# An encoder trunk on one core: the feed-forward activation transposed by Vector in one instruction per block, with SBUF-to-SBUF transfers to the quadrants

## The chip, the cores and the metric

The kernel runs on one core of a Trainium2 chip. The metric is the device time of one execution in microseconds (us), as the median over runs; a span is the time that the hardware profiler shows between the first and the last instruction of one profiled execution.

## The reference

Two layers over 256 tokens of width 2048, all in float32. Each layer is a token mixer with four kinds of heads (differential attention, convolution, grouped-query attention, neighbourhood attention) followed by a dense SwiGLU channel mixer. The change touches the channel mixer alone:

```
for l in range(DEPTH):                      # DEPTH = 2
    ...                                     # token mixer, x = x + rmsnorm(mixed)
    h = rmsnorm(x, norm_ffn_pre[l])         # x is 256 x 2048
    f = (silu(h @ ffn_gate[l]) * (h @ ffn_up[l])) @ ffn_down[l]   # hidden width 5632
    x = x + rmsnorm(f, norm_ffn_post[l])
```

The product with `ffn_down` contracts over the hidden width, so the activation `silu(gate) * up`, which comes out with tokens on the partitions, has to stand with hidden channels on the partitions before it can be a stationary operand of TensorE.

## The kernel before, in words

**Precision.** Every float32 product is made of three single-pass products: an operand is split into a high part (rounded) and a low part (the rest). ScalarE writes the high part (`whi`, `xT`, `hT`) and VectorE the low part by a subtraction (`wlo` and the second half of `xT`, `hT`). So one step, a `Step` of `products`, is six matmuls of 128 x 512 columns on two PSUM banks, and each weight tile passes through ScalarE and VectorE once.

**Units and groups.** `plan` cuts each big product into units of 128 rows by 1024 columns of weights. Two units come by one load of 1 MB into one of `NRAW` = 3 raw buffers; in the phase "gu" (gate and up) a load is two transfers of 512 KB, one from `ffn_gate` and one from `ffn_up`. Split units live in `NSPLIT` = 7 buffers `hi` and 7 buffers `lo`. Units are used in groups, four at a time as a rule: four steps for the first 128 tokens (tok 0), then the same four units for the other 128 (tok 1). A split buffer comes free with a tok-1 step. A column block of 512 hidden channels, j, is 16 units, that is 32 steps. There are 11 blocks per layer.

**Order.** Nothing reorders the program: each engine runs its instructions as the Python code emits them. `run` emits step by step: first `tick`, which advances every open generator whose planned time has come by one `yield`, then `splits_to`, which emits the splits up to 7 units beyond the units that are used up, and after every second low part the load that goes into the raw buffer which that low part was the last to read. Loads go out on SP's queue.

**Around the change.** When the last step of block j for one tok is emitted, `ffn_half` is spawned. ScalarE applies SiLU to the gate's bank (`h`), VectorE multiplies by the up bank (`h`), then `quadrants` is called four times with a `yield` after each: four VectorE transposes of 32 partitions by 128 columns a time, each of which swaps 32 x 32 blocks and writes them to another quadrant of partitions, into `ht`. After the fourth, `split_hi_lo` writes `hT[j]`: the high part by ScalarE, the low part by VectorE. `hT[j]` is read in the phase "down", which goes through the units in the order of j. The tiles `h` and `ht` come from a pool with 4 buffers.

**Transfers in the program.** The transfer of `gains` (`constants`, on ScalarE's queue) is the first of the program; on SP follow `x`, a weight load, `x`, two weight loads, two of `x`, and then the weight load that is the ninth. `load_bias` issues 16 transfers of 64 KB in a row on SP, once per layer; its destinations are separate parts of one tile.

Of the kernel before, what the change touches and what calls it, by code (L numbers as in the profile page):

```python
# [19 lines left out]
P = 128  # L20
# [30 lines left out]
class Unit:  # L51


    def __init__(self, phase, pair, k, raw, half):
        self.phase, self.pair, self.k, self.raw, self.half = phase, pair, k, raw, half
        self.hi = self.lo = None
# [46 lines left out]
class Trunk:  # L103
    def __init__(self, ctx, tc, a):
        self.tc, self.a = tc, a
        self.nc = Engines(self, tc.nc)
        self.at = {"PE": 0.0, "ACT": 0.0, "DVE": 0.0, "Pool": 0.0}
        self.chain = 0.0
        self.table = None
        self.made = {}  # L110
        pool = lambda name, bufs, **kw: ctx.enter_context(tc.tile_pool(name=name, bufs=bufs, **kw))
        self.cp = pool("consts", 1)
        self.wp = pool("weights", NSPLIT)
        self.sp = pool("slots", SLOTS)
        self.tp = pool("temps", 4)
        self.pacc = pool("acc", 4, space=PSUM)
        self.psc = pool("scores", 2, space=PSUM)
        self.ptp = pool("transposes", 2, space=PSUM)
        self.pd = pool("spill", 1, space=DRAM)
        self.open = {"sc": 0, "tp": 0}  # L120
        self.gens = []
        self.units, self.raws, self.steps = [], [], []
        self.next_raw = self.next_split = self.next_lo = 0
        self.conv_work = None
        self.xT = [None] * 4
        self.x = [None] * T
        self.acc = {}
        self.uid = 0
# [286 lines left out]


    def square_sum(self, src, out, n=(512,), bias=0.0):
        junk = self.tp.tile([P] + list(n), mybir.dt.bfloat16, tag="junk", bufs=2, name=self.name("junk"))
        self.nc.scalar.activation(junk, src, AF.Square, bias=bias, accum_out=out)

    def transpose_x(self, phase, tok, c):
# [109 lines left out]
    def ffn_half(self, phase, j, tok):  # L531
        nc = self.nc
        gate, up = (self.acc[phase, j, tok, b] for b in range(2))
        h = self.tmp([512], "h")
        r = self.rstd[:, tok:tok + 1]
        nc.scalar.activation(h, gate, AF.Silu, scale=r)
        nc.vector.scalar_tensor_tensor(h, up, r, h, op0=ALU.mult, op1=ALU.mult)
        yield
        if tok == 0:
            self.hT[j] = self.slot([2, 4, S], F32R, "hT")  # L540
        t = self.tmp([4, P], "ht")
        for q in range(4):
            self.quadrants(t, h.rearrange("p (k n) -> p k n", k=4), q)
            yield
        self.split_hi_lo([self.hT[j][:, i, :, tok * P:(tok + 1) * P] for i in range(2)], t)
        self.mark("h", phase[1], j, tok)

    def quadrants(self, dst, src, q):

        qs = slice(32 * q, 32 * q + 32)  # L550
        for r in range(4):
            rs = slice(32 * r, 32 * r + 32)
            self.nc.vector.transpose(dst[qs, :, rs], src[rs, :, qs])


    def layer_consts(self, l):
# [600 lines left out]
```

## Time and profile before

| what | value |
|---|---|
| median of 3 runs | 2179.1 us (2178.68 to 2179.65) |
| the profiled execution, its own time | 2179.21 us |
| its span | 2177.4 us |
| granted TensorE clock, mean | 0.999 of full speed |
| PE busy | 2156.2 us, 99% |
| DVE busy | 1459.9 us, 67% |
| ACT busy | 1083.2 us, 50% |
| bytes moved | 424.46 MB, 195 GB/s |

How to read it: PE is TensorE's matmuls, PEld its weight loads, DVE is VectorE, ACT ScalarE, POOL GpSimd, SP SyncE, and SPq SP's queue of transfers. A line "a<-b" gives the tile written and the tiles read. What stands in brackets behind a row of a timeline is how long the engine had been idle before it and for whom it waited. All lines of the helper that wraps the engines appear as L89.

### The profile page before, as it was taken

The numbers are of one execution on the slowest core, as the hardware profiler recorded it, in microseconds if no ns is written. First come the engines' busy times: TensorE is split into PE (matmuls) and PEld (weight loads), VectorE is DVE, ScalarE is ACT, GpSimd is POOL, SyncE is SP. The second block draws the span as 40 slices with busy tenths as digits, with TensorE's granted clock in tenths as the row PEclk, the third lists the DMA queues.
The fourth block names the chain that finished last, engine by engine and source line by source line (L and its number), as shares of the span: only waits on it lengthen the run. The fifth ranks groups of instructions, "written<-read, shape, count | busy, mean of one in ns | idle before, by whom it ended". The sixth has DMA issues, their size and how long they took to land.

```text
span 2177.4 us, 25660 instructions
## 1 busy us (share of the span) xinstructions
PE 2156.2 (99%) x9720; PEld 1780.7 (82%) x9720; DVE 1459.9 (67%) x2202; ACT 1083.2 (50%) x1420; POOL 28.7 (1%) x38
## 2 busy tenths in 40 slices
PE   8999999999999999999999999999999999999998
PEld 6888887888888888888878888878888888888886
DVE  5898555777777777444468975556677777764444
ACT  5556754544444444343465576554444444443432
POOL 0000000000000000000000000000000000000000
PEclk9999999999999999999999999999999999999999
DMA  7556446655555555555575553556555655555553
GB/s 281 197 173 181 171 148 222 210 196 193 193 194 194 193 194 194 213 193 194 211 238 186 188 186 135 208 189 222 193 191 180 209 193 193 179 208 213 193 216 132
DMA packets 170013, 424.46 MB, mean 195 GB/s; under 512 B 18593, under 2 KB 19105, under 8 KB 167585
## 3 DMA queue, kind: packets, MB, share of 16 engines
q1 hardware_dynamic: 169744, 422.79, 56.5%
q8 instruction: 76, 1.25, 0.2%
q14 instruction: 49, 0.39, 0.1%
q10 hardware_dynamic: 144, 0.03, 0.0%
HBM read 414.40 MB, written 8.39 MB: 194 GB/s over the span
## 4 chain that ended last, share of the span: by engine, by line
PE 96%; ACT 2%; DVE 1%; DMA 1%; issue 1%; SPq 0%; DVEq 0%; POOLq 0%; ACTq 0%
PE acc L89 92%; PE tp L89 3%; PE sc L89 1%; DMA raw<-in_w_in_dram 1%; ACT whi L89 1%; ACT workA L89 0%; ACT L89 0%; DVE xT L89 0%; DVE mx L89 0%; DVE wlo L89 0%; DVE x L89 0%; ACT xT L89 0%; ACT conv L89 0%; ACT qkD L89 0%; ACT junk L89 0%
## 5 line engine op out<-in xcount | busy, mean ns | idle before, releaser
L89 PE MATMUL acc<-whi,xT 128*128 128x512 f32 x4096 | 1292.9, 393 | 7.4 <-DVE xT L89 2.9
L89 PEld LDWEIGHTS acc<-whi,xT 128*128 128x128 f32 x4096 | 769.3, 188 | 172.3 <-DVE xT L89 5.5
L89 PE MATMUL acc<-wlo,xT 128*128 128x512 f32 x2048 | 798.7, 390 | 0.5 <-DVE wlo L89 0.5
L89 DVE SCALAR_TENSOR_TENSOR wlo<-raw,gains,whi 128x1024 fp32r<-128x1024 f32 x512 | 641.4, 1280 | 146.9 <-ACT whi L89 141.2
L89 ACT ACTIVATE whi<-raw,gains 128x1024 fp32r<-128x1024 f32 x512 | 574.7, 1147 | 269.6 <-PE acc L89 243.1
L89 DVE TENSOR_TENSOR wlo<-raw,whi 128x1024 fp32r<-128x1024 f32 x240 | 293.3, 1224 | 256.9 <-ACT whi L89 240.1
L89 PEld LDWEIGHTS acc<-wlo,xT 128*128 128x128 f32 x2048 | 385.1, 188 | 78.4 <-DVE wlo L89 1.0
L89 PE MATMUL acc<-whi,hT 128*128 128x512 f32 x1408 | 434.1, 389 | 0.0
L89 ACT ACTIVATE whi<-raw 128x1024 fp32r<-128x1024 f32 x240 | 253.6, 1060 | 296.1 <-PE acc L89 295.2
L89 PEld LDWEIGHTS acc<-whi,hT 128*128 128x128 f32 x1408 | 264.3, 188 | 54.9
L89 PE MATMUL acc<-wlo,hT 128*128 128x512 f32 x704 | 273.9, 389 | 0.0
L89 DVE STREAM_TRANSPOSE ht<-h 32x128 f32<-32x128 f32 x704 | 213.1, 303 | 10.9
L89 PEld LDWEIGHTS acc<-wlo,hT 128*128 128x128 f32 x704 | 132.1, 188 | 27.3
L89 ACT ACTIVATE hT<-ht 128x512 fp32r<-128x512 f32 x44 | 27.8, 632 | 244.3 <-DVE ht L89 244.3
L89 DVE SCALAR_TENSOR_TENSOR h<-acc,rstd,h 128x512 f32<-128x512 f32 x44 | 32.9, 747 | 110.8 <-ACT h L89 110.7
L89 DVE SCALAR_TENSOR_TENSOR conv<-uT,lc,conv 128x256 f32<-128x256 f32 x240 | 99.2, 477 | 0.0
L89 ACT ACTIVATE h<-acc,rstd 128x512 f32<-128x512 f32 x44 | 30.3, 688 | 81.6 <-PE acc L89 81.3
L89 DVE TENSOR_TENSOR hT<-ht,hT 128x512 fp32r<-128x512 f32 x44 | 30.4, 692 | 26.6 <-ACT hT L89 26.5
L89 ACT ACTIVATE junk<-acc 128x512 bf16<-128x512 f32 x32 | 19.1, 596 | 55.4 <-PE acc L89 53.3
L89 DVE TENSOR_TENSOR mg<-acc,gpost 128x512 f32<-128x512 f32 x32 | 21.4, 686 | 36.0 <-PE acc L89 19.3
L89 PE MATMUL acc<-whi,mixC 128*128 128x512 f32 x128 | 44.7, 402 | 0.0
L89 DVE TENSOR_TENSOR xT<-tp,xT 128x512 fp32r<-128x512 f32 x32 | 22.0, 687 | 30.2 <-ACT xT L89 30.2
(136 smaller groups left out, 992.0 us busy)
## 6 DMA issues: line engine op xcount, KB each, us to landing
raw<-in_ffn_gate_dram SPq DMA_DIRECT2D x176, 512.0 KB, 3.9
raw<-in_ffn_up_dram SPq DMA_DIRECT2D x176, 512.0 KB, 4.8
raw<-in_ffn_down_dram SPq DMA_DIRECT2D x88, 1024.0 KB, 4.9
raw<-in_w_in_dram SPq DMA_DIRECT2D x63, 1024.0 KB, 5.1
raw<-in_w_out_dram SPq DMA_DIRECT2D x32, 1024.0 KB, 5.0
raw<-in_w_in_dram SPq DMA_DIRECT2D x34, 512.0 KB, 4.8
x_spill<-x SPq DMA_DIRECT2D x6, 1024.0 KB, 7.7
x<-x_spill SPq DMA_DIRECT2D x6, 1024.0 KB, 8.4
```

The source lines that it names most:

```text
L89: return f(*args, **kw)
```

## The change

The 16 transposes per block and tok become one. It transposes each 32 x 32 block where it stands, on all 128 partitions, into a new tile `blocks` laid out by destination quadrant. Then SP issues 16 transfers, each of 32 partitions by 512 bytes (16 KB), from quadrant t of `blocks` to quadrant q of `ht`. Eight further ticks pass before the split. `ht` now has the layout (t, k, n) and the split reads it through a rearranged view. The pool `temps` gets 5 buffers in place of 4, and the scratch tile `junk` of the sums of squares 1 in place of 2.

```
-        self.tp = pool("temps", 4)
+        self.tp = pool("temps", 5)
...
-        junk = self.tp.tile([P] + list(n), mybir.dt.bfloat16, tag="junk", bufs=2, name=self.name("junk"))
+        junk = self.tp.tile([P] + list(n), mybir.dt.bfloat16, tag="junk", bufs=1, name=self.name("junk"))
...
         t = self.tmp([4, P], "ht")
-        for q in range(4):
-            self.quadrants(t, h.rearrange("p (k n) -> p k n", k=4), q)
-            yield
-        self.split_hi_lo([self.hT[j][:, i, :, tok * P:(tok + 1) * P] for i in range(2)], t)
+        yield from self.turned(t, h)
+        t = t.rearrange("p t (k n) -> p k t n", k=4)
+        dst = [self.hT[j][:, i, :, tok * P:(tok + 1) * P].rearrange("p k (t n) -> p k t n", t=4) for i in range(2)]
+        self.split_hi_lo(dst, t)
         self.mark("h", phase[1], j, tok)
 
-    def quadrants(self, dst, src, q):
-
-        qs = slice(32 * q, 32 * q + 32)
-        for r in range(4):
-            rs = slice(32 * r, 32 * r + 32)
-            self.nc.vector.transpose(dst[qs, :, rs], src[rs, :, qs])
+    def turned(self, dst, src):
+
+        nc = self.nc
+        b = self.tmp([4, P], "blocks")
+        nc.vector.transpose(b.rearrange("p q (k n) -> p k q n", k=4),
+                            src.rearrange("p (k q n) -> p k q n", k=4, q=4))
+        yield
+        for t in range(4):
+            for q in range(4):
+                nc.sync.dma_start(dst[32 * q:32 * q + 32, t], b[32 * t:32 * t + 32, q])
+        for _ in range(8):
+            yield
```

## Rows read from the trace of the kernel before

**Rows 1.** The page: busy time, TensorE's clock over 40 slices, SP's ring.

```profile
PE 2156.2 (99%) x9720; PEld 1780.7 (82%) x9720; DVE 1459.9 (67%) x2202; ACT 1083.2 (50%) x1420; POOL 28.7 (1%) x38
...
PEclk9999999999999999999999999999999999999999
...
q1 hardware_dynamic: 169744, 422.79, 56.5%
```

**Rows 2.** Busy time by stretch: gate and up, then down, first layer.

```profile
core 0: us, PE busy (x) PEld busy (x) DVE busy (x) ACT busy (x) POOL busy (x), PEclk, DMA share, GB/s
...
580.00:680.00 100.00, 100.00 (x443) 82.84 (x442) 73.70 (x121) 46.21 (x46) 0.00 (x0) 1.00 0.57 191
...
860.00:960.00 100.00, 100.00 (x443) 82.84 (x442) 50.70 (x49) 40.25 (x39) 0.00 (x0) 1.00 0.57 207
```

**Rows 3.** Waits of PE, 300 to 1100 us: total, times, longest.

```profile
PE acc L89 <- DVE xT L89: 1.4, 3, 0.6
PE acc L89 <- ACT xT L89: 0.7, 1, 0.7
```

**Rows 4.** Groups of instructions by shape: the transposes and the split behind them.

```profile
L89 DVE STREAM_TRANSPOSE ht<-h 32x128 f32<-32x128 f32 x704 | 213.1, 303 | 10.9
...
L89 DVE TENSOR_TENSOR hT<-ht,hT 128x512 fp32r<-128x512 f32 x44 | 30.4, 692 | 26.6 <-ACT hT L89 26.5
...
L89 ACT ACTIVATE hT<-ht 128x512 fp32r<-128x512 f32 x44 | 27.8, 632 | 244.3 <-DVE ht L89 244.3
```

**Rows 5.** Timeline of ACT from one block's activation to the next.

```profile
539.10 0.69 ACT L89 ACTIVATE h<-acc,rstd 128x512 f32<-128x512 f32 x1 [4.06 <-PE acc L89]
540.68 1.15 ACT L89 ACTIVATE whi<-raw,gains 128x1024 fp32r<-128x1024 f32 x1 [0.90 <-PE acc L89]
...
544.53 0.69 ACT L89 ACTIVATE h<-acc,rstd 128x512 f32<-128x512 f32 x1
...
552.54 0.63 ACT L89 ACTIVATE hT<-ht 128x512 fp32r<-128x512 f32 x1 [6.28 <-DVE ht L89]
...
582.62 0.69 ACT L89 ACTIVATE h<-acc,rstd 128x512 f32<-128x512 f32 x1 [4.06 <-PE acc L89]
```

**Rows 6.** Timeline of DVE in the same stretch.

```profile
541.68 1.24 DVE L89 STREAM_TRANSPOSE ht<-h 32x128 f32<-32x128 f32 x4
542.95 1.28 DVE L89 SCALAR_TENSOR_TENSOR wlo<-raw,gains,whi 128x1024 fp32r<-128x1024 f32 x1
...
553.20 0.69 DVE L89 TENSOR_TENSOR hT<-ht,hT 128x512 fp32r<-128x512 f32 x1 [0.70 <-ACT hT L89]
...
555.19 2.48 DVE L89 SCALAR_TENSOR_TENSOR wlo<-raw,gains,whi 128x1024 fp32r<-128x1024 f32 x2
```

**Rows 7.** Timeline of SP's queue: four weight loads' transfers.

```profile
544.26 0.37 SPq L214 DMA_DIRECT2D raw<-in_ffn_gate_dram  x1
544.67 0.47 SPq L214 DMA_DIRECT2D raw<-in_ffn_up_dram  x1
548.75 0.37 SPq L214 DMA_DIRECT2D raw<-in_ffn_gate_dram  x1
...
557.70 0.37 SPq L214 DMA_DIRECT2D raw<-in_ffn_gate_dram  x1
```

**Rows 8.** Waits of SP's queue, 0 to 12 us.

```profile
SPq L214 <- DMA gains<-in_gains_dram: 0.3, 1, 0.3
```

**Rows 9.** Timeline of SP's queue: the 16 transfers of `load_bias`, both layers.

```profile
164.28 11.89 SPq L612 DMA_DIRECT2D bias<-in_na_rpb_rev_dram  x16
...
1245.05 11.04 SPq L612 DMA_DIRECT2D bias<-in_na_rpb_rev_dram  x16
```

**Rows 10.** Transfers by line: count, KB each, median us from issue to landing.

```profile
raw<-in_ffn_gate_dram SPq DMA_DIRECT2D x176, 512.0 KB, 3.9
raw<-in_ffn_up_dram SPq DMA_DIRECT2D x176, 512.0 KB, 4.8
...
bias<-in_na_rpb_rev_dram SPq DMA_DIRECT2D x32, 64.0 KB, 4.2
...
out_dram<-x SPq DMA_DIRECT2D x8, 256.0 KB, 2.4
```

More of the change, by code (lines that the diff above doesn't have):

```diff
@@ L541, in ffn_half @@
         t = self.tmp([4, P], "ht")
-        for q in range(4):
-            self.quadrants(t, h.rearrange("p (k n) -> p k n", k=4), q)
-            yield
-        self.split_hi_lo([self.hT[j][:, i, :, tok * P:(tok + 1) * P] for i in range(2)], t)
-        self.mark("h", phase[1], j, tok)
-    def quadrants(self, dst, src, q):
-        qs = slice(32 * q, 32 * q + 32)
-        for r in range(4):
-            rs = slice(32 * r, 32 * r + 32)
-            self.nc.vector.transpose(dst[qs, :, rs], src[rs, :, qs])
+        yield from self.turned(t, h)
+        t = t.rearrange("p t (k n) -> p k t n", k=4)
+        dst = [self.hT[j][:, i, :, tok * P:(tok + 1) * P].rearrange("p k (t n) -> p k t n", t=4) for i in range(2)]
+        self.split_hi_lo(dst, t)
+        self.mark("h", phase[1], j, tok)
+    def turned(self, dst, src):
[8 more added lines that the diff above has]
+        for _ in range(8):
+            yield
     def layer_consts(self, l):
```

## The prediction

> **What bounds the kernel now.** I read busy times first, then stretches, then PE's waits. TensorE is busy 2156.2 of 2177.4 us at a granted clock of nine tenths or more in every slice [rows 1], that is 2.4 GHz, the upper of its two levels. The stretches tell more: in gate-and-up, where the transposes run, PE is busy 100.00 of 100 us with 443 matmuls; in down, which has none, it is again 100.00 with 443 [rows 2]. DVE falls from 73.70 to 50.70 between them and PE's pace does not move. So DVE's load costs PE nothing here. Last, PE's waits: from 300 to 1100 us, which holds a whole gate-and-up and most of down, two rows of 1.4 and 0.7 us, both for `xT` at the start [rows 3]; none names the activation, a weight or a transpose. PE sets the time, and this change takes no work from PE. The question is only whether what it adds can make PE wait.
>
> The profiled execution took 2179.21 us, 1.8 more than its span, and 0.1 from the median of 2179.1; the sum is made against 2179.2.
>
> **The change, part by part.**
>
> *Vector.* 704 transposes of 303 ns, 16 for each of 44 activations (4.85 us), become 44 of 128 x 512. No such instruction is in the trace. It has four times the elements per partition of the old one: at least 0.30, at most 4 x 0.303 = 1.21 us. I take 0.69, the row of the nearest DVE operation of that shape [rows 4]. DVE gives up 213.1 - 30 = 183 us. None of it reaches the end, as PE waits for no DVE work there [rows 3].
>
> *The split.* ACT's and DVE's instruction keep their shape (0.63 and 0.69 us [rows 4]) and read runs of 32 elements; even doubled, 1.3 us per activation goes into engines at 46 and 74% [rows 2].
>
> *Pools.* One scratch buffer for `junk` serializes ACT with itself, which it is already; the fifth buffer takes up `blocks`. Nothing.
>
> *Transfers.* 704, in 44 bursts of 16, on the queue that carries all weights. This is where a cost can come from, so I follow one block, with PE's finish of tok 0 at 539.10 and of tok 1 at 544.53; the next block follows at 582.62 [rows 5]. So a block takes 43.52 us, a step 43.52/32 = 1.36, a group of 8 steps 10.88.
>
> (a) Place. By the code the transpose stands where the first four stand now, behind `h` and one `wlo`, at 541.68 [rows 6]. With 0.69 in place of 1.24 the next `wlo` ends half a microsecond sooner, and the load behind it, call it L1, starts at 543.7 in place of 544.26 [rows 7]. The burst is emitted one tick later, right behind L1's two transfers: 543.7 + 0.41 + 0.51 = 544.6. It needs the transpose, done at 542.4: SP doesn't wait for DVE. Behind it: load L2 (now at 548.75), then tok 1's burst, then L3 (now at 557.70) [rows 7].
>
> (b) Pitch. Gate's transfer occupies the queue for 0.37 us and the next starts 0.41 behind it; up's takes 0.47 [rows 7]. I take 0.41, and 0.51 as the slow form. The upper bound is the `bias` burst, 16 transfers in 11.89 and 11.04 us, 0.69 to 0.74 each, with 256 short rows each against 32 here [rows 9]. The floor is 16 x 0.37 = 5.9 us per burst.
>
> (c) Semaphores. A weight load waited 0.3 us for `gains` [rows 8], with which it shares no data: it is the ninth transfer of the program, and `gains` the first. I read that as a rotation over eight semaphores: a transfer waits until the eighth before it has landed. Small transfers 7 and 8 therefore wait for L1's, which land 3.9 and 4.8 us after issue [rows 10]: 547.6 and 548.9. Number 9 waits for number 1, which lies behind L1 in the rings: I estimate 549.2. Then 9 to 16 at 0.41: the last is issued at 552.1 and off the queue by 552.5. A burst holds SP for B = 552.5 - 544.6 = 7.9 us. L2 takes 0.9 (552.5 to 553.4); tok 1's burst meets L2 as the first met L1, 553.4 to 561.3, and its last transfer, issued at 560.9, lands at 563.3 if it takes the 2.4 us of `out` (256 KB, nothing ahead of it [rows 10]).
>
> (d) Who waits. Counting ticks, tok 1's split is emitted 16 steps after tok 0 ended: on ACT before the first `whi` of the group whose splits begin at 540.68 + 2 x 10.88 = 562.4 [rows 5], on DVE before that group's first two `wlo`. If it waits, weight splits wait behind it on both. In the trace two `wlo` end 2.48 + (555.19 - 552.54) + 1.2 = 3.85 us after the split may start, counted as 0.66 to DVE's part, 0.70 for it, 2.48 for both [rows 5, 6]. The second is needed in the fourth tok-0 step: 544.53 + 3 x 1.36 + 21.76 = 570.4; the first, 2.6 us behind, at 569.0, with 0.2 more because the low part is the second matmul. The tighter of the two: landing by 566.6. Expected 563.3: 3.3 us to spare. Before, ACT stood 6.28 us at this place [rows 5] and PE never waited.
>
> (e) The weights. L3 goes out at 561.3 in place of 557.70. A load is first split 9.7 us after its undisturbed issue (10.88 later by the group rhythm, less the 1.2 of its own `wlo`), and lands 5.2 us after it (0.41 + 4.8 [rows 7, 10]): 4.5 us of slack; the split buffers hold 11 more (ten steps from a `whi` to its use, less 2.4 for both splits). Undisturbed, L3 would go at about 554.1, so it may go until 569.6. Cost nothing, as long as 544.6 + 2B + 0.9 stays below 569.6, B below 12.0: (d) decides first, with 547.5 + 2B below 566.6, B below 9.5.
>
> (f) Bandwidth. q1's packets took 56.5% of 16 engines, 116 ns each [rows 1]. 32 rows x 32 transfers add 1024 packets per block, 64 per engine, at most 7.4 of 43.5 us: the share goes from 0.57 [rows 2] to at most 0.74. Hidden.
>
> Sum: 2179.2 - 0 (DVE's 183 us lie beside PE) + 0 (bursts, 3.3 us under their limit) = 2179.2, to be compared with 2179.1.
>
> The `bias` row also bears on a rule that speaks against the change. It shows 4.2 us per landing, yet 16 in 11.0 to 11.9 us [rows 9, 10]: they overlap, up to eight at a time, so the sum goes by the pitch. The Trainium skill, "DMA: Bandwidth & Descriptors", Rules for kernel authors, wants small transfers coalesced, as under 64 KB one pays mostly overhead, and its section on the anatomy of one DMA puts the fixed part at about 2 us. Paid one after another, that would be some 2780 us as an estimate by the page; on this the row disagrees.
>
> **The rivals.**
>
> *Late landing (slower).* The small transfers take 4.2 us as `bias` does, at a pitch of 0.51. Then 16 waits for 8 (548.9 + 4.2), B = 553.1 + 0.5 - 544.6 = 9.0, the last lands at 544.6 + 18 + 0.9 - 0.5 + 4.2 = 567.2: 0.6 us late, in 22 blocks 13 us, 2192. For it: weight loads are always in the rings. Against: the burst's second half has none ahead of it. At 1.2 us late it is 26 us, 2205.
>
> *The queue as the bound (slower).* The pitch is that of `bias`, 0.69 to 0.74. B = 11.04 to 11.89, beyond 9.5 by 1.5 to 2.4, twice per block: 3 to 4.7 us x 22 = 66 to 103 us, 2245 to 2282. For it: the only burst of 16 in the trace. Against: eight times the rows per transfer, and gate's transfers with 256 rows take only 0.37 [rows 7]. It decides from a pitch of 0.6.
>
> *One after another (slower).* SP gets no overlap from short transfers, each 2.4 us as `out` [rows 10]: 32 x 2.4 = 77 us, and eight loads x 0.9 = 7, against 43.5 us per block: 40.5 x 22 = 891 us, 3070. Against: the overlap of `bias` [rows 9]. (This is the rule named above, with a row's price.)
>
> *Vector was on the path (faster).* All that PE waits for from 300 to 1100 us is 2.1 us, per layer; both gone, 4 us, 2175, just beyond 0.2%. Against: those waits are for `xT`, before the first transpose.
>
> **How the numbers follow.** A difference under 0.2% (4.4 us) can't be told from none in this kernel. Forecast, no change: 0.68. Late landing 0.13, bias's pitch 0.12, one after another 0.04, Vector on the path 0.03. Same 0.68; slower 0.13 + 0.12 + 0.04 = 0.29; faster 0.03. The range runs from 2175 to 2205, the slow end of late landing: 0.68 + 0.13 = 0.81 inside. The forecast's own range is 2175 to 2183.
>
> **What would show it.** After: DVE's busy time near 1277 us; 44 transposes of 0.3 to 1.2 us; 704 issues on SP of about 0.4 us; bursts of some 8 us; no row of PE waiting for `whi` or `wlo` in gate-and-up; 443 matmuls per 100 us there; ACT's waits for `hT` now ended by a transfer, and at most as long as before. Wrong would be: bursts over 9.5 us, landings of small transfers over 4 us, ACT held at `hT` beyond 566.6 on this block's clock, PE waiting for `wlo` once per block.

## The result, and the profile after

The changed kernel takes 2218.38 us as the median of 4 runs (2216.27 to 2220.57), the kernel before 2179.06: 39.3 us slower, a ratio of 1.018 (95% interval 1.0163 to 1.0198). The forecast was 2179.2 with a range to 2205, so it was wrong.

The page after: busy time, and the shares of the chain that ended last, by engine and by line (L557 is the line of the small transfers).

```profile
PE 2170.2 (98%) x9720; PEld 1784.5 (80%) x9720; DVE 1270.4 (57%) x1542; ACT 1093.0 (49%) x1420; POOL 28.7 (1%) x38
...
PE 67%; SPq 17%; DVE 5%; DMA 4%; issue 3%; ACT 3%; ACTq 0%; DVEq 0%; POOLq 0%
PE acc L89 63%; SPq L557 16%; DVE wlo L89 4%; PE tp L89 3%; SPq L214 2%; DMA ht<-blocks 1%; PE sc L89 1%; DMA raw<-in_ffn_up_dram 1%; DMA raw<-in_w_in_dram 1%; ACT h L89 1%; DVE hT L89 1%; ACT whi L89 1%; ACT hT L89 0%; DMA raw<-in_ffn_gate_dram 0%; ACT workA L89 0%
```

DVE gave up the work about as reckoned, 1459.9 to 1270.4 us [rows 1] where 1277 was expected. But SP's queue now has 17% of the chain. The stretches say where: two of gate-and-up, then one of down.

```profile
core 0: us, PE busy (x) PEld busy (x) DVE busy (x) ACT busy (x) POOL busy (x), PEclk, DMA share, GB/s
...
480.00:580.00 100.00, 96.93 (x425) 79.24 (x424) 50.25 (x48) 43.70 (x44) 0.00 (x0) 1.00 0.59 199
580.00:680.00 100.00, 97.89 (x431) 80.36 (x430) 54.49 (x50) 47.30 (x46) 0.00 (x0) 1.00 0.64 214
...
860.00:960.00 100.00, 100.00 (x443) 82.81 (x442) 48.34 (x44) 40.65 (x41) 0.00 (x0) 1.00 0.58 209
```

In gate-and-up PE now does 425 and 431 matmuls in 100 us where it did 443 [rows 2]; down is untouched. PE's waits for `wlo` over the whole span (total, times, longest), before and after:

```profile
PE acc L89 <- DVE wlo L89: 0.5, 1, 0.5
```

```profile
PE acc L89 <- DVE wlo L89: 27.1, 21, 2.6
```

Of the 21 waits after, 20 lie in the two layers' gate-and-up, 26.5 us in all, one in each of 20 of its 22 blocks.

The profiled execution's span grew by 2218.8 - 2177.4 = 41.4 us: PE's idle time by 27.4 and PE's busy time by 14.0 (2170.2 - 2156.2). The last section comes to the 14.0.

**One block, followed.** The timeline of SP's queue, with PE's end of tok 0 at 545.93:

```profile
550.41 0.37 SPq L214 DMA_DIRECT2D raw<-in_ffn_gate_dram  x1
550.82 0.47 SPq L214 DMA_DIRECT2D raw<-in_ffn_up_dram  x1
551.34 10.86 SPq L557 DMA_DIRECT2D ht<-blocks  x16
562.31 0.52 SPq L214 DMA_DIRECT2D raw<-in_ffn_gate_dram  x1
562.87 0.47 SPq L214 DMA_DIRECT2D raw<-in_ffn_up_dram  x1
563.43 10.02 SPq L557 DMA_DIRECT2D ht<-blocks  x16
573.55 0.53 SPq L214 DMA_DIRECT2D raw<-in_ffn_gate_dram  x1
```

The order is the one forecast: L1, burst, L2, burst, L3. But a burst holds the queue 10.0 to 10.9 us, not 7.9. The instructions by tile give the reason (duration in ns: least, median, most; the second row is the time to landing in us):

```profile
L557 SPq DMA_DIRECT2D ht<-blocks x704: 507/589/1703, 415.7 to 1990.7; - x176
...
DMA to landing us min/median/max: 1.7/1.8/4.9
```

Each transfer occupies SP 0.589 us and the next one starts 0.64 us after it (10.02 / 16, with the gap). They land in 1.8 us, sooner than the 2.4 us of the forecast. What follows on ACT and on DVE:

```profile
545.93 0.69 ACT L89 ACTIVATE h<-acc,rstd 128x512 f32<-128x512 f32 x1 [1.62 <-PE acc L89]
...
574.90 0.63 ACT L89 ACTIVATE hT<-ht 128x512 fp32r<-128x512 f32 x1 [6.18 <-DMA ht<-blocks]
```

```profile
575.57 0.69 DVE L89 TENSOR_TENSOR hT<-ht,hT 128x512 fp32r<-128x512 f32 x1 [8.17 <-ACT hT L89]
576.18 2.47 DVE L89 SCALAR_TENSOR_TENSOR wlo<-raw,gains,whi 128x1024 fp32r<-128x1024 f32 x2
```

and on PE:

```profile
577.51 0.50 PE L89 MATMUL acc<-wlo,xT 128*128 128x512 f32 x1 [1.24 <-DVE wlo L89]
```

Read the rows backwards. PE waits for a `wlo` that DVE started at 576.18. DVE had been idle 8.17 us before the low part of `hT`, whose ACT half stood 6.18 us until the last small transfer landed. The prediction's limit for that landing was 566.6 with tok 0 ended at 539.10, that is 27.5 us after it: here 573.4. The split started at 574.90, 1.5 us late, and PE waited 1.24. In this block the limit held; the landing missed it.

While the later part of a burst is issued the transfer engines are nearly idle. The same kernel's 540 to 585 us in 40 slices, busy tenths and GB/s:

```profile
DMA  9999499400799301110028991100112899999998
GB/s 404 370 371 330 115 319 408 182 0 0 147 390 399 77 21 29 29 42 16 15 29 229 406 337 32 29 22 22 29 29 33 218 404 397 399 384 397 366 255 288
```

The two runs of slices at 15 to 42 GB/s are the bursts, from where the weight load ahead of each has landed. It is SP's queue that is taken, not the engines or the rings.

### The profile page after: what moved, and what is told of

Its sections match the earlier page's. It is cut to its first block, busy times and chain, and to the rows that moved or that the text cites. A ratio compares the mean times of both kernels' runs of the same rounds, so it can differ in the third digit from the quotient of the medians.

```text
span 2218.8 us, 26032 instructions
## 1 busy us (share of the span) xinstructions
PE 2170.2 (98%) x9720; PEld 1784.5 (80%) x9720; DVE 1270.4 (57%) x1542; ACT 1093.0 (49%) x1420; POOL 28.7 (1%) x38
## 4 chain that ended last, share of the span: by engine, by line
PE 67%; SPq 17%; DVE 5%; DMA 4%; issue 3%; ACT 3%; ACTq 0%; DVEq 0%; POOLq 0%
PE acc L89 63%; SPq L557 16%; DVE wlo L89 4%; PE tp L89 3%; SPq L214 2%; DMA ht<-blocks 1%; PE sc L89 1%; DMA raw<-in_ffn_up_dram 1%; DMA raw<-in_w_in_dram 1%; ACT h L89 1%; DVE hT L89 1%; ACT whi L89 1%; ACT hT L89 0%; DMA raw<-in_ffn_gate_dram 0%; ACT workA L89 0%
## 5 line engine op out<-in xcount | busy, mean ns | idle before, releaser
L89 PE MATMUL acc<-wlo,xT 128*128 128x512 f32 x2048 | 804.5, 393 | 27.1 <-DVE wlo L89 27.1
L89 DVE SCALAR_TENSOR_TENSOR wlo<-raw,gains,whi 128x1024 fp32r<-128x1024 f32 x512 | 640.1, 1277 | 184.6 <-ACT whi L89 183.2
L89 PEld LDWEIGHTS acc<-wlo,hT 128*128 128x128 f32 x704 | 132.1, 188 | 27.5
L89 ACT ACTIVATE h<-acc,rstd 128x512 f32<-128x512 f32 x44 | 30.3, 688 | 41.4 <-PE acc L89 41.1
L89 PE MATMUL acc<-whi,mixB 128*128 128x512 f32 x128 | 42.2, 397 | 0.0
L89 PE MATMUL acc<-whi,mixD 128*128 128x512 f32 x128 | 41.6, 391 | 0.0
```

The costliest lines, as they stand in the source:

```text
L89: return f(*args, **kw)
```

## The experiments

Two theories were told apart first. **Theory A, late activation:** ACT and DVE stand at the split of `hT` until the burst has landed, and the weight splits queue behind them. **Theory B, late weights:** the loads that stand behind the bursts reach ACT too late, wherever the split stands. Each experiment is an edit of the changed kernel, compared with the kernel before on the same chip.

**1. The split later.**

```
-        for _ in range(8):
+        for _ in range(24):
             yield
```

> 24 ticks in place of 8 between the transfers and the split; transfers, bursts and loads stay as they are. Theory A (late activation: ACT and DVE stand at the split of hT until the burst has landed, and the weight splits queue behind them): the burst has landed long before, ACT's wait for ht falls from 190 us to near 0, PE's waits for wlo from 27 us to under 3, time 2178 to 2184. Theory B (late weights: the loads that stand behind the bursts on SP reach ACT too late, wherever the split stands): loads go out as late as now, time stays at 2210 to 2222.

Measured: 2182.79 us, ratio 1.0021 (1.0011 to 1.0031). PE's waits for `wlo` fell to 1.3 us and ACT no longer waits for `ht`. So A holds for nearly all of the 39 us. What is left, 3.7 us, is not zero, and ACT's waits for `ffn_up` loads rose to 381 us, from 12.3 in the kernel before and 128.0 in the changed one:

```profile
ACT whi L89 <- DMA raw<-in_ffn_up_dram: 381.1, 113, 10.4
```

The weights are late too. That they nearly use up the lead of the split buffers is a reading of these rows, not shown by a run of its own.

**2. Nobody waits for the transfers.**

```
-        yield from self.turned(t, h)
+        t = yield from self.turned(t, h)     # turned ends with "return b"
```

> The split reads blocks itself in place of ht, so that nothing waits for the 16 transfers, which are still issued at the same place (the quadrants are left unmoved in the result). Theory A: nothing is held at the split, 2178 to 2184, although SP is held 10 us per burst as now. Theory B: 2210 to 2222, with PE waiting for wlo about 27 us.

Measured: 2179.25 us, ratio 1.0001 (0.9992 to 1.0010). The bursts are as long as before (11.40 and 10.05 us in one block), 704 transfers move the same bytes, and the time is that of the kernel before. ACT's waits for `ffn_up` loads rose here too, to 292.6 us, at no cost. Transfers, bandwidth and the held queue alone cost nothing; the wait at the split does.

**3 to 6. The number of transfers.** Twelve and fourteen:

```
         for t in range(4):
+            if t < 2:                                   # t == 0 for fourteen
+                for q in range(2):
+                    nc.sync.dma_start(dst[64 * q:64 * q + 64, t], b[64 * t:64 * t + 64, q])
+            else:
                 for q in range(4):
```

Twenty and eighteen:

```
+                for c in (slice(0, 64), slice(64, 128)) if t == 0 else (slice(0, 128),):   # eighteen: t == 0 and q < 2
+                    nc.sync.dma_start(dst[32 * q:32 * q + 32, t, c], b[32 * t:32 * t + 32, q, c])
```

> 12 transfers in place of 16: half of the data goes by four transfers of 64 partitions, the other half by eight of 32 (the blocks of the first half land in other quadrants than they should). At 0.64 us each a burst is 7.7 us, under the limit of 9.5 that the prediction worked out for 16. Theory A with that limit: no waits of PE for wlo, 2178 to 2184. If the time follows the number of transfers without a limit: 12/16 of the 39 us, 2208.

> 14 transfers in place of 16: two of 64 partitions for one source quadrant (its blocks land in other quadrants than they should), twelve of 32 for the others. At 0.64 us each a burst is 9.0 us, just under the limit of 9.5. Theory A: 2178 to 2186. If the limit lies lower, at 12 transfers: half of the 39 us, about 2200.

> 18 transfers in place of 16: two of those of one source quadrant are cut in two. Theory A with the slope that 16 and 20 transfers gave, (2364.0 - 2218.4) / 4 = 36.4 us per transfer: 2291 (2275 to 2310). A cost that grows as the square of the excess over the limit would give less, about 2270.

> 20 transfers in place of 16: those of one source quadrant are cut in two of 256 bytes per row. At 0.64 us each a burst is 12.9 us. Theory A: each transfer more delays the second burst's end by 2 x 0.64 us per block, 22 x 4 x 1.28 = 113 us over the changed kernel, 2330 (2290 to 2350). If the time follows the number of transfers without a limit: 20/16 of 39 us, 2228.

| transfers | a burst, shortest and mean of 44, us | PE's waits for wlo, us | PE busy, us | mean clock | median, us | ratio (95%) |
|---|---|---|---|---|---|---|
| 12 | 7.5, 7.8 | 0.5 | 2157.1 | 0.999 | 2179.22 | 1.0000 (0.9991 to 1.0010) |
| 14 | 8.7, 9.0 | 0.5 | 2156.7 | 0.999 | 2179.79 | 1.0003 (0.9993 to 1.0013) |
| 16, the change | 10.0, 10.3 | 27.1 | 2170.2 | 0.995 | 2218.38 | 1.018 (1.0163 to 1.0198) |
| 18 | 11.3, 11.7 | 79.4 | 2207.0 | 0.976 | 2307.37 | 1.0587 (1.0571 to 1.0603) |
| 20 | 12.5, 12.9 | 136.1 | 2208.3 | 0.963 | 2364.02 | 1.0842 (1.0824 to 1.0860) |

The rows of PE's waits for eighteen and twenty:

```profile
PE acc L89 <- DVE wlo L89: 79.4, 23, 5.3
```

```profile
PE acc L89 <- DVE wlo L89: 136.1, 23, 7.6
```

There is a limit, and it lies between 9.0 and 10.3 us per burst (means), where the prediction put 9.5. Beyond it PE's waits grow by (136.1 - 27.1) / 4 = 27.3 us per transfer; 22 blocks x 2 x 0.64 = 28.2 was the working. Twenty came out above its range of 2290 to 2350, a miss, and eighteen inside its own, 2275 to 2310: the waits follow the theory, and the rest is PE's busy time, which grew almost wholly between 16 and 18.

**7. No transfers.**

```
-        for t in range(4):
-            for q in range(4):
-                nc.sync.dma_start(dst[32 * q:32 * q + 32, t], b[32 * t:32 * t + 32, q])
         for _ in range(8):
             yield
+        return b
```

> No transfers at all: the split reads blocks directly (the quadrants are left unmoved in the result), eight ticks as before. It is the change's gain alone, DVE relieved of 183 us. Theory A says that DVE was not on the path: 2178 to 2181, the kernel before. Rival (DVE's relief is worth time, which the transfers eat up): under 2174.

Measured: 2179.21 us, ratio 1.0000 (0.9990 to 1.0009), with DVE at 1275.8 us in place of 1459.9. Relieving DVE of 184 us is worth nothing.

**8. The shape of a transfer.**

```
-                nc.sync.dma_start(dst[32 * q:32 * q + 32, t], b[32 * t:32 * t + 32, q])
+                nc.sync.dma_start(dst[:, t, 32 * q:32 * q + 32], b[:, q, 32 * t:32 * t + 32])
```

> 16 transfers of 16 KB as now, but each of all 128 partitions by 128 bytes in place of 32 partitions by 512 bytes (the blocks land elsewhere than they should). Question: what makes a transfer hold SP 0.59 us in the burst, when a weight transfer holds it 0.37 to 0.47. If it is the partitions under 128 (bias with 64 had 0.6 too): 0.4 to 0.5 us each, bursts of 7 to 8.5 us, and by theory A's limit of 9.5 no wait, 2178 to 2186. If it is that the transfer stands in a row of transfers between places in SBUF, whatever its shape: 0.59 each, bursts of 10 us, 2210 to 2225.

Measured: 2222.84 us, ratio 1.0200 (1.0184 to 1.0215), the second answer:

```profile
L557 SPq DMA_DIRECT2D ht<-blocks x704: 464/599/1917, 414.9 to 1991.6; - x176
```

All 128 partitions, a quarter of the bytes per row, and still 0.599 us. The few partitions are not what makes a transfer slow to issue.

**9. The source of a transfer.**

```
-                nc.sync.dma_start(dst[32 * q:32 * q + 32, t], b[32 * t:32 * t + 32, q])
+                src = self.a["ffn_gate"][0][32 * t:32 * t + 32, q * P:(q + 1) * P]
+                nc.sync.dma_start(dst[32 * q:32 * q + 32, t], src)      # the split reads blocks
```

> The 16 transfers keep their shape and place but read 32 rows of 512 bytes of a weight in DRAM in place of blocks, into ht that nobody reads; the split reads blocks (the quadrants are left unmoved in the result). Question: does the place of the source make the 0.59 us per transfer. If SBUF as a source makes it: 0.37 to 0.47 us each, bursts of 6.5 to 8.3 us. If each transfer in a row of small ones takes it, from wherever: 0.59 each, 10 us. Time 2178 to 2184 either way, as nothing waits for them.

Measured: 2179.3 us, ratio 1.0001 (0.9990 to 1.0013), and

```profile
L558 SPq DMA_DIRECT2D ht<-in_ffn_gate_dram x704: 310/419/1782, 414.6 to 1945.7; - x176
```

0.419 us in place of 0.589 with the destination, the size and the place in the queue unchanged; experiment 2, where nobody waits for the transfers either, also has 0.589. The source in SBUF makes this difference. It isn't the source alone that counts: the `bias` burst reads DRAM too and holds SP longer, with 64 KB in 256 rows per transfer (kernel before):

```profile
L612 SPq DMA_DIRECT2D bias<-in_na_rpb_rev_dram x32: 595/615/1227, 164.3 to 1255.5; - x32
```

The bursts shrank less than the transfers, to 9.50 and 8.48 us in one block, above the 8.3 that was expected at most: 16 x (0.419 + 0.04) is 7.3, some transfers took up to 1.78 us, and SP now waited inside the bursts until weight loads had landed, 45.9 us in all for those of `ffn_up`, where the changed kernel has 0.4:

```profile
SPq L558 <- DMA raw<-in_ffn_up_dram: 45.9, 40, 1.6
```

```profile
SPq L557 <- DMA raw<-in_ffn_up_dram: 0.4, 1, 0.4
```

**10. Two queues.**

```
-                nc.sync.dma_start(dst[32 * q:32 * q + 32, t], b[32 * t:32 * t + 32, q])
+                queue = nc.sync if t < 2 else nc.queue          # nc.queue is ScalarE's; q is now the outer loop
+                queue.dma_start(dst[32 * q:32 * q + 32, t], b[32 * t:32 * t + 32, q])
```

> Eight of the 16 transfers go out on ScalarE's queue, eight on SP's. If each queue has its own pace of 0.64 us, SP is held 5.1 us per burst and ACT 4.7 us, the last landing comes 5 us sooner than now, and by theory A nothing waits at the split; ACT's own 5 us stand where it has 11 us of lead: 2178 to 2186. If the 0.59 us per transfer is a pace that both queues share, each queue is held some 10 us as now, ACT too: 2220 or more.

Measured: 2248.65 us, ratio 1.0315 (1.0297 to 1.0332). The time of the second answer, but not by its mechanism. A transfer still holds its own queue about as long as before (median 0.588 us on SP, 0.602 on ACT), yet eight on ACT took 5.8 and 8.0 us:

```profile
549.98 5.81 ACTq L558 DMA_DIRECT2D ht<-blocks  x8
555.89 1.15 ACT L89 ACTIVATE whi<-raw,gains 128x1024 fp32r<-128x1024 f32 x1 [5.13 <-DMA raw<-in_ffn_gate_dram]
...
560.25 7.95 ACTq L558 DMA_DIRECT2D ht<-blocks  x8
568.30 2.19 ACT L89 ACTIVATE whi<-raw,gains 128x1024 fp32r<-128x1024 f32 x2 [9.64 <-DMA ht<-blocks]
```

The weight splits stand behind the issues on the same engine, and PE waits for `whi` 22.1 us and for `wlo` 18.4. ACT's split of `hT` itself hardly waits (1.0 us in all). SP's bursts of eight took 8.45 and 4.94 us in the same block. What makes them long is waiting for transfers that have yet to land: SP's waits at the small transfers come to 153 us in all, 1.6 in the changed kernel, nearly all of them for small transfers and for weight loads:

```profile
SPq L558 <- DMA ht<-blocks: 84.4, 79, 2.7
SPq L558 <- DMA raw<-in_ffn_gate_dram: 58.1, 20, 3.3
```

On ACT the last of the second eight starts 2.3 us after the seventh has ended; for what it waits no row names.

**11. The split four steps later.**

```
-        for _ in range(8):
+        for _ in range(12):
             yield
```

> 12 ticks in place of 8 between transfers and split, with bursts of 10 us as now. Tok 1's split then stands four steps (5.4 us) later, behind the first weight splits of its group on ACT, where the next ones have 11 us of lead in place of 5.5. Theory A: no waits of PE for wlo, 2178 to 2184, and without the 3.7 us that 24 ticks cost. If the lateness of the weights alone costs those 3.7 us, 2182 to 2184 as with 24 ticks.

Measured: 2194.48 us, ratio 1.0071 (1.0056 to 1.0086): a miss of both. ACT's wait for the transfers is gone, yet DVE still stands, because ACT's half of the split now stands behind a `whi` whose load is late. ACT, then DVE:

```profile
564.60 1.15 ACT L89 ACTIVATE whi<-raw,gains 128x1024 fp32r<-128x1024 f32 x1 [7.58 <-DMA raw<-in_ffn_up_dram]
565.65 0.61 ACT L89 ACTIVATE hT<-ht 128x512 fp32r<-128x512 f32 x1
```

```profile
566.30 0.69 DVE L89 TENSOR_TENSOR hT<-ht,hT 128x512 fp32r<-128x512 f32 x1 [7.96 <-ACT hT L89]
566.91 2.47 DVE L89 SCALAR_TENSOR_TENSOR wlo<-raw,gains,whi 128x1024 fp32r<-128x1024 f32 x2
```

PE waits for `wlo` 8.7 us in 14 pieces. So theory A in its pure form is too narrow. What costs, by these rows, is anything late in front of the split on ACT, as DVE waits with it; the burst makes two things late, the landing and the loads behind it. In the change it is the landing, here the load, with 24 ticks nearly neither.

**12. Twelve transfers with the whole computation.**

```
+            nc.vector.transpose(dst[rs, t].rearrange("p (k n) -> p k n", k=4),      # rs: rows 32t to 32t + 32
+                                src.rearrange("p (k q n) -> p k q n", k=4, q=4)[rs, :, t])
             for q in range(4):
-                nc.sync.dma_start(dst[32 * q:32 * q + 32, t], b[32 * t:32 * t + 32, q])
+                if q != t:
+                    nc.sync.dma_start(dst[32 * q:32 * q + 32, t], b[rs, q])
```

> The four quadrants that stay where they are (t = q) are transposed straight into ht by VectorE (four more transposes of 32 x 128, 1.2 us), 12 transfers carry the others. The whole computation is done. Bursts of 12 x 0.64 = 7.7 us as with 12 transfers above: 2178 to 2182, the kernel before.

Measured: 2179.25 us, ratio 1.0000 (0.9991 to 1.0010), bursts of 7.48 and 7.54 us, PE's waits for `wlo` 0.5 us. The quadrants that stay need no transfer; without them the change costs nothing. No version tried is faster than the kernel before.

## Why the prediction was wrong

*PE as the bound, DVE off the path:* right. Experiment 7 relieves DVE of 184 us without any transfer and the time doesn't move. The transpose took 705 ns, 690 were taken.

*The places (a), the weights' slack (e), the bandwidth (f):* the order on SP's queue was as worked out, and the first burst left 5.4 us after tok 0's end where 5.5 was worked out. The bandwidth was free (experiment 2), though (f) counted 32 packets per transfer and the trace has 48. Of the weights it was said that they don't decide first; that holds for the change, but in experiments 1 and 11, where the split stands later and ACT waits for loads, the kernel is still 3.7 and 15 us slower than before.

*The pitch (b):* this is the step that failed. 0.41 us was taken, 0.51 as the slow form, both from weight transfers that read DRAM; it is 0.64. So in the block followed the second burst landed 1.5 us after (d)'s limit, where 3.3 us to spare had been worked out, and PE waited. The only burst in the trace before, `bias` at 0.69 to 0.74, had been set aside because of its short rows [rows 9]. The price was taken from the weight loads' rows, when the other burst came closer to it. That closeness is in part luck: `bias` reads DRAM, and experiment 9 shows that for small transfers a source in SBUF is worth 0.17 us each; there was no row for it.

*The semaphores (c):* the waits that (c) worked out are hardly there in the change, 1.6 us over all 44 bursts: at 0.64 us the eighth transfer back has mostly landed. At a pitch near the assumed one they are: in experiment 9, with 0.46, SP waited 56 us inside the bursts for weight loads to land, some 1.3 us per burst.

*The limit (d):* right as far as the runs can tell: 9.5 us per burst worked out, between 9.0 and 10.3 found, with 27.3 us per transfer beyond it where 28.2 was worked out. One sum in it is written wrongly: 2.48 + (555.19 - 552.54) + 1.2 is 6.33, and the 3.85 that the limit goes by is that of the three terms named behind it, 0.66 + 0.70 + 2.48. The landing was taken at 2.4 us; with the 1.8 measured the limit moves from 9.5 to 9.8. As an estimate from that, the mean burst of 10.3 us gives 2 x 0.5 x 22 = 22 us of waiting, where PE waited 27. The rival "the queue as the bound" described what happened and named the pitch from which it decides, 0.6; it was given 0.12, at the price of `bias`'s pitch. The range ended at 2205 because that rival was left outside it. So the mechanism was worked out rightly and the size of one term, the pitch, was not.

The rule that the prediction quoted against the change, from the Trainium skill, "DMA: Bandwidth & Descriptors", Rules for kernel authors (coalesce small transfers), was right in its direction: twelve are free and twenty cost 185 us. The Trainium skill's fixed part of about 2 us, which the same page gives for transfers issued by GpSimd, is near the landing of 1.8 us that SP's transfers show here. But it was neither this nor any lack of overlap that decided; it was the 0.59 us for which each transfer holds the issuing queue. The same page of the Trainium skill, under "Issuing engines are not separate DMA queues", says that issuing from several engines saves only the sequencer's time, which is usually small. Here that time, 0.59 us of issue beside 1.8 us to landing, makes the cost, and experiment 10 shows that another engine's queue is no free place for it.

## What to carry to other kernels

An in-order queue that carries a steady stream has a limit for what may be put between two of its loads, and time beyond the limit goes straight to the end. Work out that limit from the code and the timeline, then take the price per transfer from a burst of the same kind, or, where there is none, count the range up to the price of the worst burst that there is. Ask of each consumer what else stands behind it on its engine: a split that waits for a transfer holds every weight split behind it. And before building around a limit, look for transfers that needn't be made.

## What the runs showed of the hardware that was not expected

**The source counts.** Sixteen transfers in a row hold SP 0.589 us each from SBUF to SBUF, 0.599 with another shape, 0.419 from DRAM to SBUF; the quickest of the 704 in the changed kernel took 0.507. But `bias`, from DRAM as well, took 0.615 with larger transfers of more rows, so the source is one part of the price and not all of it. What in the issue takes longer wasn't found.

**PE's clock falls after some of the waits.** Two stretches of 10 us in the changed kernel; PE's first wait in gate-and-up begins at the end of the first and ends in the second:

```profile
430.00:440.00 10.00, 9.47 (x42) 7.51 (x40) 0.93 (x2) 2.41 (x3) 0.00 (x0) 1.00 0.29 80
440.00:450.00 10.00, 8.65 (x31) 6.99 (x32) 7.46 (x7) 5.43 (x6) 0.00 (x0) 0.83 1.01 361
```

```profile
441.35 0.50 PE L89 MATMUL acc<-wlo,xT 128*128 128x512 f32 x1 [1.88 <-DVE wlo L89]
...
443.94 0.63 PE L89 MATMUL acc<-whi,xT 128*128 128x512 f32 x1
444.37 0.63 PE L89 MATMUL acc<-wlo,xT 128*128 128x512 f32 x1
...
446.03 0.39 PE L89 MATMUL acc<-whi,xT 128*128 128x512 f32 x1
446.26 0.39 PE L89 MATMUL acc<-wlo,xT 128*128 128x512 f32 x1
```

After 1.88 us of waiting PE's matmuls start 0.43 us apart for a while, then 0.23 again: the lower level of 1.2 GHz and the upper of 2.4. The mean granted clock in these 10 us is 0.83. Five such places in the changed kernel, among 20 waits, cost 8.5 us together (the sum of one minus the clock over the 10-us stretches below 0.995), beside the 14.0 us by which PE's busy time grew; the rest of the 14.0 wasn't traced. The length of the wait alone doesn't tell: after a wait of 2.08 us, which ended at 1814.37, the clock stayed at 1.00. With 18 and 20 transfers, whose waits are up to 5.3 and 7.6 us long, PE's busy time grew by 51 and 52 us. So a wait of PE can cost more than it lasts, and the price per transfer beyond the limit is 36 us in the medians (16 to 20) where the waits alone make 27. It isn't even: 44.5 us per transfer from 16 to 18, where PE's busy time grew by 37, and 28.3 from 18 to 20, where it grew by 1.
